# SSD exponentials queued behind ScalarE's last evacuation, and modulation rows in buffers of their own

## The chip, the core and the metric

One NeuronCore of a Trainium2 chip runs the whole kernel. Its engines are TensorE (PE, matrix products; PEld is its weight load), VectorE (DVE), ScalarE (ACT), GpSimd (POOL) and SyncE (SP, which here only issues DMAs). Each works through its own queue in order and waits on semaphores of the others. The metric is the device time of one execution in microseconds (us), less is better.

## The reference

Two layers over 512 latent and 256 context tokens of width 1024. Layer 0 mixes tokens by gated linear attention (GLA), layer 1 by a Mamba-2 scan (SSD) with 8 groups of 4 heads; each is followed by a squared-ReLU MLP (FFN), and each sub-layer is modulated by shift, scale and gate that come from the conditioning vectors.

```python
def sq_relu_mlp(h, w1, w2):
    return jnp.square(jax.nn.relu(h @ w1)) @ w2

def ssd_chunk_scan(xs, dt, a, bm, cm, s0):
    ...
    def step(s, inp):
        xi, dti, bi, ci = inp
        cum = jnp.cumsum(dti * a, axis=1)
        seg = cum[:, :, None] - cum[:, None, :]
        decay = jnp.exp(jnp.where(mask, seg, -jnp.inf))
        xdt = xi * dti[..., None]
        cb = jnp.einsum('bign,bjgn->bijg', ci, bi)
        y = jnp.einsum('bijg,bijgr,bjgrp->bigrp', cb, decay, xdt)
        y = y + jnp.einsum('bign,bigr,bgrpn->bigrp', ci, jnp.exp(cum), s)
        ...

def reference(...):
    ...
    s_lat = jax.nn.silu(c)
    s_ctx = jax.nn.silu(c_ctx)
    for i in range(DEPTH):
        m_l = jnp.split((s_lat @ ada_w[i] + ada_b[i])[:, None, :], 6, axis=-1)
        m_c = jnp.split(s_ctx @ ada_w[i] + ada_b[i], 6, axis=-1)
        ul = snake(modulate(hl, m_l[0], m_l[1]))
        ...
        hl = layer_norm(DEEPNORM_ALPHA * hl + m_l[2] * snake(yl), ln_g[i, 0], ln_b[i, 0])
        hl = layer_norm(DEEPNORM_ALPHA * hl + m_l[5] * sq_relu_mlp(modulate(hl, m_l[3], m_l[4]), ffn_w1[i], ffn_w2[i]),
                        ln_g[i, 1], ln_b[i, 1])
```

## The kernel before

Activations stand transposed, 128 features to a partition and up to 768 tokens along a row. A large product (`prod`, L250) splits both operands in a high and a low part and adds three products, so one output block of 128 features takes 8 slices of depth times 3 matmuls for each token segment. A block's weights come by a DMA of 512 KB into a raw tile (`wload`, L237), ScalarE casts the high part (L203, `wh`) and VectorE subtracts for the low part (L204, `wl`). The raw tiles are one pool of four buffers.

A scheduler orders the instructions of each engine when the kernel is built, by the order of the program and by when it expects operands to be ready; on the chip every engine keeps that order. Two lists of generators are woven into the products: `worked()` counts the columns that `prod` has sent, and every 768 of them it makes a step of `side`, and every `pace[0]` such units a step of `background`.

The **background** work is `ada_rows`. For a modulation vector (layer, m) it takes eight blocks; for each it loads 512 KB of the modulation weights (L154) into a raw tile, and VectorE multiplies it by the conditioning row and sums along the row (L157), twice where context and latent tokens both need it (the first result then goes to a junk tile). These raw tiles were taken from the weights' four buffers. 24 such loads belong to the GLA stage and 56 to the first FFN.

The **FFN** runs in blocks of eight hidden slices: `f1` makes a product, ScalarE takes the relu out of PSUM (L394) and squares it (L396), GpSimd squares it in full precision (L395, `rq`), VectorE subtracts (L397, `rl`); then `accum_proj` makes eight products of the block with the second weight matrix and VectorE adds each to the accumulators (L431). The gate for that addition comes from the rows.

The **SSD** layer runs over eight groups. For a group, `group(g)` makes the products of B, C and two x blocks, each followed by `conv` (evacuation of PSUM by ScalarE at L887 and L889, start of the conv at L894, four taps on VectorE at L896, tanh at L898), then two gate products (`gate_tiles`, tanh at L919). The scan of the group before (`inner`) is a `side` generator and goes in between. It

- copies B and x to natural layout by transposes (L906) and copies on ScalarE (L907, `Bn`, `xnat`);
- weights x with the decays on VectorE (L961, `xw`) and makes chunk states (L973), and the C-B products with a copy on ScalarE (L995, `cbs`);
- loads decay rows for a chunk of 128 tokens and both directions (L939, tile `L`, ten buffers), masks them on GpSimd (L941), takes 4 exponentials on each tile on ScalarE (L1028, function `decays`), adds both directions on GpSimd (L1031), multiplies by `cbs` on VectorE (L1032) and makes the outputs on TensorE (L1039).

The loads, masks and exponentials depend on nothing of the group but its decay rows, so the scheduler was free to place them far ahead.

Of the kernel before, what the change touches and what calls it, by code (L numbers as in the profile page):

```python
# [9 lines left out]
F32 = mybir.dt.float32  # L10
# [6 lines left out]
P = 128  # L17
D = 1024
# [42 lines left out]
def tile_backbone(ctx, tc, xT, cc, cr, vecs, rows, ada_w0, ada_wr, lnf, ffn_w1, ffn_w2,  # L61
# [81 lines left out]
    def ada_rows(items, alloc, junk):  # L143
        srow = [alloc(s) for s in range(2)]
        for s in range(2):
            nc.sync.dma_start(srow[s], cr[s:s + 1, :].to_broadcast([P, D]))
            nc.scalar.activation(srow[s], srow[s], AF.Silu)
        for layer, m in items:
            streams = range(1 if layer and m > 1 else 2)
            t = ct([P, 8, 2], f"row{layer}{m}")  # L150
            nc.gpsimd.memset(t, 0.0)
            for b in range(8):
                raw = raw_tile()
                nc.sync.dma_start(raw, ada_wr[48 * layer + 8 * m - 16 + b])  # L154
                for s in streams:
                    o = raw if s == streams[-1] else junk()
                    nc.vector.scalar_tensor_tensor(o, raw, 1.0, srow[s], ALU.mult, ALU.mult, accum_out=t[:, b, s:s + 1])  # L157
                yield
            c0 = V_ADA + 48 * layer + 8 * m
            nc.vector.tensor_tensor(t, t, vec[:, c0:c0 + 8].unsqueeze(2).to_broadcast([P, 8, 2]), ALU.add)  # L160
            mods[layer, m] = t
# [211 lines left out]
    def ffn(layer, xs, acc, segs, pool, npre, presegs, restsegs, passes, after):  # L373
        W1, W2 = ffn_w1[layer], ffn_w2[layer]
        rs = {}
        NN = span(segs)[1]

        def f1(m, sg, hold=None):
            w, ps = hold or (weights(W1, m), mm_ps(sg))
            prod(ps, w, xs, sg, KT)  # L380
            f1_out(m, ps)

        def f1_out(m, ps):
            if m not in rs:
                rs[m] = (pool.tile([P, NN], F32R, tag="rs", name=nm("rh"), bufs=20),
                         pool.tile([P, NN], F32R, tag="rs", name=nm("rl"), bufs=20))
            rh, rl = rs[m]
            for piece in passes if m == DFF // P - 1 else (segs,):
                a, b = span(piece)
                eng = nc.gpsimd if piece is segs else nc.vector  # L390
                r = pool.tile([P, NN], F32, tag="rr", name=nm("rr"), bufs=2)
                q = pool.tile([P, NN], F32, tag="rq", name=nm("rq"), bufs=1)
                for (t0, n, _) in piece:
                    nc.scalar.activation(r[:, t0:t0 + n], part_of(ps, t0, n), AF.Relu)  # L394
                eng.tensor_mul(q[:, a:b], r[:, a:b], r[:, a:b])  # L395
                nc.scalar.activation(rh[:, a:b], r[:, a:b], AF.Square)  # L396
                nc.vector.tensor_sub(rl[:, a:b], q[:, a:b], rh[:, a:b].bitcast(F32))  # L397

        nlast = NN // 256
        h0 = 0  # L400
        for bi, nb in enumerate((8, 8, 8, 8 - nlast, nlast)):
            ms = range(h0, h0 + nb)
            if bi == 0:
                drain(1)
                held = []
                for m in ms[:npre]:
                    held.append((weights(W1, m), mm_ps(segs)))
                    prod(held[-1][1], held[-1][0], xs, presegs, KT)
                drain()
                for m in ms[:npre]:  # L410
                    f1(m, restsegs, held[m])
                pace[0] = 11
                ms = ms[npre:]
            if bi == 4:
                ws = pair_weights(W2, h0, nb,
                                  lambda j: [pool.tile([P, NN], F32R, tag="rs", name=nm("ws"), bufs=20) for _ in range(2)])
            for m in ms:
                f1(m, segs)
            ys = [rs[m] for m in range(h0, h0 + nb)]
            if bi == 0:  # L420
                gate = mod(layer, 5)
                pace[0] = 22
            if bi < 4:
                accum_proj(W2, h0, nb, ys, gate, acc, segs)
            else:
                accum_last(ws, ys, gate, acc, passes, after, early=None if layer == 0 else 5)
            h0 += nb
# [44 lines left out]
    def gla_layer(xs, first):  # L472
# [17 lines left out]
        def wk(shape, name):  # L490
            return gp.tile(shape, F32, tag="wk", name=nm(name), bufs=3)

        background.append(ada_rows([(0, 2), (0, 3), (0, 4)], lambda s: xn_tile(f"srow{s}"), raw_tile))
        pace[0] = 12
        aT = gp.tile([P, NT], F32R, tag="aT", name="aT")
        a2 = gp.tile([P, 2, 512], F32R, tag="a2", name="a2")
# [265 lines left out]
    def ssd_layer(xs, accd, acc0):  # L762
# [117 lines left out]
        def conv(j, segs):  # L880
            ps = held[1] if j == 16 else project(16 + j, segs)
            pre = pres[0]
            pres.reverse()
            c = sp.tile([P, NT + 2], F32, tag="cv", name=nm("cv"), bufs=1)
            f = apool.tile([P, NT], F32, tag="acc", name=nm("cf"))
            n = 512 if len(segs) == 1 else NT + 2
            nc.scalar.copy(pre[:, 2:514], ps[0])  # L887
            if len(segs) > 1:
                nc.scalar.copy(pre[:, 516:772], ps[1][:, 0:NCTX])  # L889

            def cw(t):
                return cvec[:, 32 * t + j:32 * t + j + 1]

            nc.scalar.activation(c[:, 0:n], pre[:, 2:2 + n], AF.Identity, bias=cw(5), scale=cw(2))  # L894
            for t in (0, 1, 3, 4):
                nc.vector.scalar_tensor_tensor(c[:, 0:n], pre[:, t:t + n], cw(t), c[:, 0:n], ALU.mult, ALU.add)  # L896
            for t0, t1, d in ((0, 512, 0), (512, 768, 2)) if len(segs) > 1 else ((0, 512, 0),):
                nc.scalar.activation(f[:, t0:t1], c[:, t0 + d:t1 + d], AF.Tanh)  # L898
                nc.vector.scalar_tensor_tensor(f[:, t0:t1], f[:, t0:t1], 1.0, c[:, t0 + d:t1 + d], ALU.add, ALU.mult)
            return f  # L900

        def natural(f, dst):
            for c0, c1 in ((0, 4), (4, 6)):
                pt = sm_ps([P, 4, P])
                for c in range(c0, c1):
                    nc.tensor.transpose(pt[:, c - c0, :], f[:, c * P:(c + 1) * P], ident)  # L906
                nc.scalar.copy(dst[:, c0:c1, :], pt[:, 0:c1 - c0, :])  # L907

        def group(g):
            fB = conv(16 + g, BOTH)  # L910
# [4 lines left out]
            def gate_tiles():  # L915
                for i in range(2):
                    z = sp.tile([P, NL], F32, tag="zs", name=nm("zs"), bufs=4)
                    zp = project(2 * g + i, LAT)[0]
                    nc.scalar.activation(z, zp, AF.Tanh, scale=0.5)  # L919
                    nc.vector.scalar_tensor_tensor(z, z, 1.0, zp, ALU.add, ALU.mult)  # L920
                    zs.append(z)

# [4 lines left out]
        def inner(g, fB, fC, fx, zs):  # L927
# [119 lines left out]
            for c in range(NLC + 1):  # L1047
# [2 lines left out]
                    outputs(c - 1, Ms.pop(c - 1))  # L1050
                if c < NLC:
                    L = Rs.pop(c)
                    decays(c, L)
                    Ms[c] = masks(c, L)
                if c + 2 < NLC:
                    Rs[c + 2] = chunk_rows(c + 2)
# [268 lines left out]
```

## Time and profile before

| | us |
|---|---|
| median of 3 runs (lowest to highest) | 1975.5 (1969.12 to 1980.79) |
| the profiled execution | 1972.94 |
| its span, first to last instruction | 1971.2 |
| TensorE busy in the span | 1882.0 |
| VectorE, ScalarE, GpSimd busy | 1260.5, 801.5, 414.6 |
| mean granted TensorE clock | 0.985 |

In a row of the profile `L1028 ACT ACTIVATE L<-L,lcol ... x4 [3.94 <-POOL L L941]` four instructions of line 1028 ran on ScalarE, which had stood idle for 3.94 us before them until line 941 on GpSimd had written tile L. PEclk is the clock that TensorE was granted, as a share of full speed. A DMA's time goes from issue to landing. By time the stages are about: the start and GLA to 450 us, the first FFN to 1050, the SSD layer to 1590, and the second FFN.

### The profile page before, as it was taken

What the parts mean: (1) busy time and instruction counts of PE and PEld (TensorE: products, weight loads), DVE (VectorE), ACT (ScalarE), POOL (GpSimd) and SP (SyncE); (2) the same over time, 40 slices, a digit from 0 to 9 for tenths busy, and PEclk for the clock granted to TensorE, in tenths of its full rate; (3) what the DMA queues carried; (4) which work ended last, traced back from release to release, by engine and by line L of the source; (5) the groups of instructions that cost most, each with busy time, mean ns of one, the idle gap of its engine ahead of it and who ended that gap; (6) DMA issues with size and microseconds to landing.
All of it is one profiled execution on the core that took longest, in us unless ns stands there. A gap on an engine that the chain in (4) does not pass through costs nothing.

```text
span 1971.2 us, 28815 instructions
## 1 busy us (share of the span) xinstructions
PE 1882.0 (95%) x11365; PEld 1607.1 (82%) x11365; DVE 1260.5 (64%) x1932; ACT 801.5 (41%) x1387; POOL 414.6 (21%) x363
## 2 busy tenths in 40 slices
PE   7989999999999999999998799999999999999997
PEld 5978888788788888888987677777787788888886
DVE  4797887888854444324478778787897673333335
ACT  3435456454213113122367645565443453323231
POOL 1123241202002002010004523334221221102012
PEclk9999999999999999999999899999999999999999
DMA  8423213124654444213134333344324423333321
GB/s 327 153 62 122 87 57 104 48 72 129 202 150 140 129 134 131 70 46 108 44 109 119 129 116 97 102 133 134 97 90 137 146 81 104 97 98 97 98 83 63
DMA packets 78999, 219.07 MB, mean 111 GB/s; under 512 B 11088, under 2 KB 15824, under 8 KB 78864
## 3 DMA queue, kind: packets, MB, share of 16 engines
q1 hardware_dynamic: 78864, 217.24, 35.3%
q8 instruction: 89, 1.46, 0.3%
q14 instruction: 46, 0.38, 0.1%
HBM read 209.07 MB, written 8.13 MB: 110 GB/s over the span
## 4 chain that ended last, share of the span: by engine, by line
PE 63%; DVE 15%; ACT 6%; issue 5%; DMA 5%; POOL 5%; SPq 0%; DVEq 0%; POOLq 0%; ACTq 0%
PE mm L250 54%; DMA L<-crowc 3%; DVE cv L896 2%; POOL L L1031 1%; DVE A L605 1%; PE sm L973 1%; DVE wl L204 1%; PE sm L688 1%; DVE E L616 1%; DVE raw L157 1%; PE mm L532 1%; ACT xn L325 1%; ACT wh L203 1%; ACT L L1028 1%; DVE lnst L315 1%
## 5 line engine op out<-in xcount | busy, mean ns | idle before, releaser
L250 PE MATMUL mm<-xh,wl 128*128 128x512 f32 (+1 forms) x1800 | 545.6, 356 | 8.3 <-DVE wl L204 8.3
L250 PE MATMUL mm<-xh,wh 128*128 128x512 f32 (+1 forms) x1800 | 548.8, 359 | 1.3 <-ACT xh L1073 1.1
L250 PE MATMUL mm<-xl,wh 128*128 128x512 f32 (+1 forms) x1800 | 546.1, 356 | 2.4 <-DVE xl L1074 2.4
L203 ACT CAST wh<-raw 128x1024 fp32r<-128x1024 f32 (+3 forms) x225 | 226.1, 1006 | 642.7 <-PE mm L250 590.6
L204 DVE TENSOR_TENSOR wl<-raw,wh 128x1024 fp32r<-128x1024 f32 (+3 forms) x225 | 276.0, 1228 | 166.8 <-ACT wh L203 163.5
L250 PEld LDWEIGHTS mm<-xh,wl 128*128 128x128 f32 x1800 | 300.9, 190 | 57.6 <-DVE wl L204 9.9
L250 PEld LDWEIGHTS mm<-xh,wh 128*128 128x128 f32 x1800 | 301.8, 190 | 53.1 <-issue 4.5
L250 PEld LDWEIGHTS mm<-xl,wh 128*128 128x128 f32 x1800 | 300.6, 190 | 52.1 <-DVE xl L1074 4.3
L395 POOL TENSOR_TENSOR rq<-rr 128x768 f32<-128x768 f32 (+1 forms) x62 | 104.7, 1689 | 735.3 <-ACT rr L394 731.4
L250 PE MATMUL mm<-rl,wh 128*128 128x512 f32 x704 | 212.5, 355 | 4.0 <-DVE rl L397 4.0
L250 PE MATMUL mm<-rh,wl 128*128 128x512 f32 x704 | 212.3, 355 | 0.0
L250 PE MATMUL mm<-rh,wh 128*128 128x512 f32 x704 | 212.0, 354 | 0.0
L431 DVE SCALAR_TENSOR_TENSOR acc<-mm,row,acc 128x256 f32<-128x256 f32 (+1 forms) x182 | 100.7, 580 | 164.1 <-PE mm L250 163.7
L157 DVE SCALAR_TENSOR_TENSOR raw<-raw,srow 128x1024 f32<-128x1024 f32 x104 | 128.7, 1242 | 85.7 <-DMA raw<-in_ada_wr_dram 84.9
L896 DVE SCALAR_TENSOR_TENSOR cv<-pre,cvec,cv 128x770 f32<-128x770 f32 (+1 forms) x128 | 135.9, 1062 | 13.0 <-ACT cv L894 11.4
L250 PEld LDWEIGHTS mm<-rl,wh 128*128 128x128 f32 x704 | 116.3, 189 | 23.3 <-DVE rl L397 4.3
L250 PEld LDWEIGHTS mm<-rh,wl 128*128 128x128 f32 x704 | 116.5, 189 | 19.0
L250 PEld LDWEIGHTS mm<-rh,wh 128*128 128x128 f32 x704 | 116.3, 188 | 19.0
L1028 ACT ACTIVATE L<-L,lcol 128x128 f32<-128x128 f32 x256 | 81.7, 392 | 64.9 <-POOL L L941 64.9
L397 DVE TENSOR_TENSOR rl<-rq,rh 128x768 fp32r<-128x768 f32 (+2 forms) x67 | 53.2, 795 | 70.7 <-POOL rq L395 69.1
L941 POOL TENSOR_SCALAR_AFFINE_SELECT L<-L 128x512 f32<-128x512 f32 x64 | 57.2, 898 | 167.3 <-DMA L<-crowc 165.4
L898 ACT ACTIVATE cf<-cv 128x512 f32<-128x512 f32 (+1 forms) x56 | 27.6, 533 | 85.7 <-DVE cv L896 85.5
(295 smaller groups left out, 2536.1 us busy)
## 6 DMA issues: line engine op xcount, KB each, us to landing
raw<-in_ffn_w_dram SPq DMA_DIRECT2D x112, 512.0 KB, 3.7
raw<-in_ada_wr_dram SPq DMA_DIRECT2D x80, 512.0 KB, 3.7
raw<-in_ssd_w_in_dram SPq DMA_DIRECT2D x48, 512.0 KB, 3.9
L<-crowc SPq DMA_DIRECT2D x64, 256.0 KB, 3.6
raw<-in_ada_w_dram SPq DMA_DIRECT2D x16, 512.0 KB, 9.2
raw<-in_gla_w_in_dram SPq DMA_DIRECT2D x16, 512.0 KB, 3.5
ec<-crow SPq DMA_DIRECT2D x64, 128.0 KB, 3.0
acc<-in_xT_dram SPq DMA_DIRECT2D x14, 384.0 KB, 6.9
```

Source lines behind the costliest of these rows:

```text
L157: nc.vector.scalar_tensor_tensor(o, raw, 1.0, srow[s], ALU.mult, ALU.mult, accum_out=t[:, b, s:s + 1])
L203: nc.scalar.copy(h, src)
L204: nc.vector.tensor_sub(l, src, h.bitcast(F32))
L250: nc.tensor.matmul(part_of(ps, t0, n), a[:, k, :], b[:, t0:t0 + n], start=(k == 0 and i == 0), stop=(k == kt - 1 and i == 2))
L315: nc.vector.bn_stats(st[:, h], ps)
L395: eng.tensor_mul(q[:, a:b], r[:, a:b], r[:, a:b])
L397: nc.vector.tensor_sub(rl[:, a:b], q[:, a:b], rh[:, a:b].bitcast(F32))
L431: nc.vector.scalar_tensor_tensor(acc[m][:, t0:t0 + n], part_of(ps, t0, n), gate[:, m, s:s + 1], (src or acc)[m][:, t0:t0 + n], ALU.mult, A ...
L896: nc.vector.scalar_tensor_tensor(c[:, 0:n], pre[:, t:t + n], cw(t), c[:, 0:n], ALU.mult, ALU.add)
L898: nc.scalar.activation(f[:, t0:t1], c[:, t0 + d:t1 + d], AF.Tanh)
L941: nc.gpsimd.affine_select(out=L[z], in_=L[z], compare_op=ALU.is_ge, fill=NEG, base=0, pattern=[[0, 4], [1 - 2 * z, P]], channel_multiplier ...
L1028: nc.scalar.activation(t[:, h, :], t[:, h, :], AF.Exp, bias=lcol[:, c, r:r + 1])
```

## The change

The rows get a tag of their own with three buffers (`rawa`, 12 KB of each partition), and each row's load is issued one row ahead; a first load stands ahead of the loop with a yield behind it. The pace of the background in the first block of the FFN goes from 11 to 15. GLA's junk tile moves to the new tag as well. In the SSD layer the evacuations at L887, L907 and L919 are remembered in `evac`, and the exponentials of a chunk are issued inside `tc.issue_after(...)`, which makes the scheduler put them behind the remembered instruction on their engine; this is an edge of order only, on the same engine.

```diff
+        def load(layer, m, b):
+            raw = wpool.tile([P, D], F32, tag="rawa", name=nm("rawa"), bufs=3)
+            nc.sync.dma_start(raw, ada_wr[48 * layer + 8 * m - 16 + b])
+            return raw
+
+        todo = [(layer, m, b) for layer, m in items for b in range(8)]
+        raws = [load(*todo.pop(0))]
+        yield
         for layer, m in items:
...
             for b in range(8):
-                raw = raw_tile()
-                nc.sync.dma_start(raw, ada_wr[48 * layer + 8 * m - 16 + b])
+                if todo:
+                    raws.append(load(*todo.pop(0)))
+                raw = raws.pop(0)
...
-                pace[0] = 11
+                pace[0] = 15
...
-        background.append(ada_rows([(0, 2), (0, 3), (0, 4)], lambda s: xn_tile(f"srow{s}"), raw_tile))
+        background.append(ada_rows([(0, 2), (0, 3), (0, 4)], lambda s: xn_tile(f"srow{s}"), lambda: wpool.tile([P, D], F32, tag="rawa", name=nm("junk"), bufs=3)))
...
-            nc.scalar.copy(pre[:, 2:514], ps[0])
+            evac[0] = nc.scalar.copy(pre[:, 2:514], ps[0])
...
+        evac = [None]
+
         def natural(f, dst):
...
-                nc.scalar.copy(dst[:, c0:c1, :], pt[:, 0:c1 - c0, :])
+                evac[0] = nc.scalar.copy(dst[:, c0:c1, :], pt[:, 0:c1 - c0, :])
...
-                    nc.scalar.activation(z, zp, AF.Tanh, scale=0.5)
+                    evac[0] = nc.scalar.activation(z, zp, AF.Tanh, scale=0.5)
...
-                    decays(c, L)
+                    with tc.issue_after(evac[0].ins):
+                        decays(c, L)
```

On ScalarE, at the turn to the second group's scan (the same `cbs_10415` in both), the exponentials of later groups (`L_11410`, `L_11419`) stood between the natural copies before:

```order
695 L907 COPY xnat_10318<-sm_10331 128x4x128
696 L907 COPY xnat_10318<-sm_10337 128x2x128
697 L1028 ACTIVATE L_11410<-L_11410,lcol 128x128 x4
698 L907 COPY xnat_10318<-sm_10355 128x4x128
699 L907 COPY xnat_10318<-sm_10361 128x2x128
700 L1028 ACTIVATE L_11419<-L_11419,lcol 128x128 x4
701 L995 COPY cbs_10415<-sm_10410 128x512
```

Now the copies run through, and the group's own first exponentials (`L_10297`) stand behind the evacuation of the C conv (`pre_9454<-mm_10468`); the changed kernel's line numbers are 9 to 12 higher:

```order
672 L918 COPY xnat_10318<-sm_10355 128x4x128
673 L918 COPY xnat_10318<-sm_10361 128x2x128
674 L1006 COPY cbs_10415<-sm_10410 128x512
675 L212 CAST wh_10650<-raw_10648 128x1024
676 L896 COPY pre_9453<-mm_10283 128x512
677 L898 COPY pre_9453<-mm_10284 128x256
678 L903 ACTIVATE cv_10449<-pre_9453,cvec 128x770
679 L907 ACTIVATE cf_10450<-cv_10449 128x512
680 L907 ACTIVATE cf_10450<-cv_10449 128x256
681 L896 COPY pre_9454<-mm_10468 128x512
682 L1039 ACTIVATE L_10297<-L_10297,lcol 128x128 x4
683 L903 ACTIVATE cv_10523<-pre_9454,cvec 128x512
```

What moved: exponentials for groups two further on gave way to those of the group itself, some ten places later.

On SyncE, whose queue issues the loads, at the start of the first FFN, weights (`in_ffn_w`) and rows (`in_ada_wr`) took turns before:

```order
102 L237 DMA raw_4709<-in_ffn_w_dram 128x1024
103 L154 DMA raw_4725<-in_ada_wr_dram 128x1024
104 L154 DMA raw_4752<-in_ada_wr_dram 128x1024
105 L146 DMA srow_4583<-in_cr_dram 128x1024
106 L146 DMA srow_4584<-in_cr_dram 128x1024
107 L237 DMA raw_4784<-in_ffn_w_dram 128x1024
108 L154 DMA raw_4796<-in_ada_wr_dram 128x1024
```

Now:

```order
105 L246 DMA raw_4851<-in_ffn_w_dram 128x1024
106 L246 DMA raw_4926<-in_ffn_w_dram 128x1024
107 L246 DMA raw_5001<-in_ffn_w_dram 128x1024
108 L146 DMA srow_4583<-in_cr_dram 128x1024
109 L146 DMA srow_4584<-in_cr_dram 128x1024
110 L150 DMA rawa_4761<-in_ada_wr_dram 128x1024
111 L150 DMA rawa_4813<-in_ada_wr_dram 128x1024
112 L150 DMA rawa_4865<-in_ada_wr_dram 128x1024
```

What moved: seven weight loads (four more stand ahead of these) now go out before the row loads of this piece, of which the first three had gone out earlier.

On VectorE, in the accumulation of the FFN's first block, from one product's accumulation (L431) to the next, before:

```order
600 L431 SCALAR_TENSOR_TENSOR acc_3243<-mm_5491,row_4589,acc_3243 128x512
601 L431 SCALAR_TENSOR_TENSOR acc_3243<-mm_5492,row_4589,acc_3243 128x256
602 L204 TENSOR_TENSOR wl_5682<-raw_5679,wh_5681 128x1024
603 L157 SCALAR_TENSOR_TENSOR raw_5922,row_5728<-raw_5922,srow_4583 128x1024
604 L431 SCALAR_TENSOR_TENSOR acc_3958<-mm_5554,row_4589,acc_3958 128x512
```

and now:

```order
604 L440 SCALAR_TENSOR_TENSOR acc_3239<-mm_5407,row_4654,acc_3239 128x512
605 L440 SCALAR_TENSOR_TENSOR acc_3239<-mm_5408,row_4654,acc_3239 128x256
606 L213 TENSOR_TENSOR wl_5601<-raw_5598,wh_5600 128x1024
607 L166 SCALAR_TENSOR_TENSOR rawa_6453,row_6451<-rawa_6453,srow_4583 128x1024
608 L166 SCALAR_TENSOR_TENSOR rawa_6510,row_6451<-rawa_6510,srow_4583 128x1024
609 L166 SCALAR_TENSOR_TENSOR rawa_6567,row_6451<-rawa_6567,srow_4583 128x1024
610 L166 SCALAR_TENSOR_TENSOR rawa_6624,row_6451<-rawa_6624,srow_4583 128x1024
611 L440 SCALAR_TENSOR_TENSOR acc_3242<-mm_5470,row_4654,acc_3242 128x512
```

What moved: four row operations stand between two accumulations, where one stood before; the rows are through earlier.

## The prediction

> **What bounds the kernel now.** I read the page's busy table first, then the chain that ended last, then TensorE's waits, and then the stretches in which those waits lie.
>
> ```profile
> span 1971.2 us, 28815 instructions
> PE 1882.0 (95%) x11365; PEld 1607.1 (82%) x11365; DVE 1260.5 (64%) x1932; ACT 801.5 (41%) x1387; POOL 414.6 (21%) x363
> PE 63%; DVE 15%; ACT 6%; issue 5%; DMA 5%; POOL 5%; SPq 0%; DVEq 0%; POOLq 0%; ACTq 0%
> ```
>
> TensorE (PE) is the bound: idle for only 1971.2 − 1882.0 = 89 us. What a change to the other engines can win is in that idle time, and in time at a lowered clock behind it. TensorE's waits, by what ended them:
>
> ```profile
> PE sm L973 <- DVE xw L961: 14.6, 6, 3.5
> PE sm L1039 <- issue: 8.6, 1, 8.6
> PE sm L586 <- DVE E L616: 8.3, 10, 3.3
> PE mm L250 <- DVE wl L204: 8.3, 5, 3.6
> PE mm L250 <- DVE rl L397: 4.0, 1, 4.0
> PE sm L715 <- ACT on L693: 3.2, 3, 2.3
> ```
>
> The columns are total us, times, longest. The first two lie in the SSD groups, L204 and L397 in the first FFN, L586 and L715 in the GLA. The stretches (us, busy time and instructions of each engine, granted clock, DMA share, GB/s): seven group periods from the first copy of the C-B products (L995) to the eighth, one such period alone, the start of the first FFN in two pieces, and the GLA stage.
>
> ```profile
> core 0: us, PE busy (x) PEld busy (x) DVE busy (x) ACT busy (x) POOL busy (x), PEclk, DMA share, GB/s
> 1069.17:1502.23 433.06, 403.32 (x2215) 325.30 (x2213) 354.97 (x523) 228.39 (x476) 146.80 (x109) 0.97 0.36 113
> 1386.84:1442.81 55.97, 55.97 (x319) 45.95 (x319) 49.20 (x72) 29.07 (x58) 17.09 (x12) 1.00 0.35 109
> 448.00:525.00 77.00, 69.35 (x406) 60.81 (x405) 69.03 (x109) 27.88 (x47) 16.49 (x8) 0.97 0.54 172
> 525.00:575.00 50.00, 50.00 (x285) 44.04 (x284) 30.62 (x50) 5.93 (x6) 0.00 (x0) 0.98 0.55 163
> 60.00:450.00 390.00, 368.77 (x2902) 328.66 (x2901) 322.40 (x512) 202.93 (x328) 97.31 (x94) 0.99 0.28 87
> ```
>
> A mean group takes 433.06/7 = 61.9 us; the second row is a group that had no wait and full clock, 55.97 us, with VectorE (DVE) at 49.20 as second bound. So there is a floor near 56 us, and the kernel has already reached it once.
>
> **Part 1: the exponentials behind an evacuation.** Rows of ScalarE (ACT), then VectorE and TensorE, at a steady group's turn:
>
> ```profile
> 1137.08 1.28 ACT L1028 ACTIVATE L<-L,lcol 128x128 f32<-128x128 f32 x4 [3.94 <-POOL L L941]
> 1138.26 0.83 ACT L907 COPY xnat<-sm 128x512 f32<-128x512 f32 x2
> 1139.12 2.60 DVE L961 TENSOR_TENSOR xw<-xnat,wc 128x256 f32<-128x256 f32 x6 [6.24 <-ACT xnat L907]
> 1140.53 2.07 PE L973 MATMUL sm<-xw,Bn 128*128 128x512 f32 x3 [3.32 <-DVE xw L961]
> ```
>
> Four exponentials of a group further on stand ahead of a natural-layout copy, wait 3.94 us for their masked tile from GpSimd (POOL), and the copy, the six products of VectorE and TensorE's L973 wait in a row behind them. At the first group it is a pile:
>
> ```profile
> 1086.68 1.28 ACT L1028 ACTIVATE L<-L,lcol 128x128 f32<-128x128 f32 x4 [4.66 <-POOL L L941]
> 1090.02 1.28 ACT L1028 ACTIVATE L<-L,lcol 128x128 f32<-128x128 f32 x4 [2.06 <-POOL L L941]
> 1093.44 0.99 ACT L1028 ACTIVATE L<-L,lcol 128x128 f32<-128x128 f32 x3 [2.14 <-POOL L L941]
> 1095.16 0.56 ACT L887 COPY pre<-mm 128x512 f32<-128x512 f32 x1
> 1098.27 1.12 PE L1039 MATMUL sm<-L,xnat 128*64 128x128 f32 x8 [8.60 <-issue]
> ```
>
> Each set waits for its own tile, the evacuation of the conv product (L887) waits behind them all, and TensorE stands 8.60 us. The change ties every exponential of the group under work behind the evacuation issued last; the new order has the natural copies and the C-B copy in one run and the exponentials behind the evacuation of the C conv. Both waits lose their cause: 14.6 + 8.6 = 23.2 us. The clock went with them: (1 − 0.97) × 433.06 = 13.0 us. Together **−36.2 us**, leaving (433.06 − 36.2)/7 = 56.7 a group, the floor that the gapless group shows.
>
> What the clock charges, and from which gap on, is in two rows more, a piece with a gap of 1.72 us and one with gaps of 0.69 and 2.34:
>
> ```profile
> 1126.00:1136.00 10.00, 8.28 (x55) 7.22 (x53) 6.53 (x6) 6.28 (x16) 7.75 (x5) 1.00 0.40 128
> 163.50:173.50 10.00, 6.97 (x34) 5.93 (x34) 7.32 (x13) 4.05 (x10) 3.31 (x3) 0.83 0.42 148
> ```
>
> 1.72 us left the clock at 1.00; 2.34 us cost (1 − 0.83) × 10 = 1.7 us more. So a gap above about 2.3 us costs itself and 1.7 or more. [...]
>
> What is late next? The moved exponentials now sit on the way to the first outputs (L1039) of their group. From the end of the C conv's product the way is: evacuation, 4 exponentials, the conv's start (L894), 4 exponentials, the add on GpSimd, the mask on VectorE. The rows (groups of instructions from 1145 to 1442 us, shapes kept apart; total us and mean ns of one, then idle time ahead):
>
> ```profile
> L887 ACT COPY pre<-mm 128x512 f32<-128x512 f32 x20 | 11.5, 576 | 0.0
> L894 ACT ACTIVATE cv<-pre,cvec 128x512 f32<-128x512 f32 x5 | 4.1, 819 | 4.7 <-DVE cf L899 4.7
> L1031 POOL TENSOR_TENSOR L<-L,L 128x512 f32<-128x512 f32 x19 | 32.6, 1714 | 16.8 <-ACT L L1028 16.8
> L1032 DVE TENSOR_TENSOR L<-L,cbs 128x512 f32<-128x512 f32 x20 | 13.6, 681 | 0.0
> L898 ACT ACTIVATE cf<-cv 128x512 f32<-128x512 f32 x20 | 12.7, 633 | 67.4 <-DVE cv L896 67.4
> ```
>
> 0.58 + 1.28 + 0.82 + 1.28 + 1.71 + 0.68 = 6.35 us, and about 7.4 with the tanh of the B conv (0.63 and 0.4 for its short half) ahead on ScalarE. In the new order 40 matmuls of the next conv cover it: a product of 48 matmuls at full rate takes 8.3 us (later pieces of the FFN hold 290 matmuls in 50 us, 0.172 each), so 40 take 6.9 us. The wait is between 0 and, if VectorE is late with its taps too, 1.5 us a group. I take 0.5, since the sum of rows is within 0.5 of the cover at both ends: +3.5 over seven groups, **SSD −32.7**, bounds −36.2 and −36.2 + 7 × 1.5 = −25.7. VectorE also waits at that mask and has 56 − 49.2 = 6.8 us a group to spare for it. GpSimd's adds of T (L1018) now stand ahead of the adds of L, and SyncE's loads of L fall later, into buffers that have been free for a group; both are inside the sum above. If this cover is gone, each us of chain costs 7.
>
> In the last group nothing follows for the exponentials to hide under but the output product; 0 to 3 us, inside the bounds.
>
> **Part 2: rows with buffers of their own, pace 15.** In the first FFN, weights and modulation rows shared four buffers, and the casts of weights (L203) waited for loads issued late, with relu evacuations (L394) behind:
>
> ```profile
> 473.10 1.05 ACT L203 CAST wh<-raw 128x1024 fp32r<-128x1024 f32 x1 [6.31 <-DMA raw<-in_ffn_w_dram]
> 469.39 1.01 PE L250 MATMUL mm<-xh,wl 128*128 128x512 f32 x2 [3.63 <-DVE wl L204]
> 523.57 1.01 PE L250 MATMUL mm<-rl,wh 128*128 128x512 f32 x2 [4.02 <-DVE rl L397]
> ```
>
> In the new order seven weight loads go out ahead of the rows and the weight's subtraction (L204) stands two places earlier on VectorE. Both waits go: 3.63 + 4.02, and the clock, 0.03 × 77 + 0.02 × 50 = 3.3: −10.95 at most. Against it, the rows are now bunched: four to a product in the accumulation, where before it was one. Their prices:
>
> ```profile
> L157 DVE SCALAR_TENSOR_TENSOR raw<-raw,srow 128x1024 f32<-128x1024 f32 x104 | 128.7, 1242 | 85.7 <-DMA raw<-in_ada_wr_dram 84.9
> L431 DVE SCALAR_TENSOR_TENSOR acc<-mm,row,acc 128x256 f32<-128x256 f32 (+1 forms) x182 | 100.7, 580 | 164.1 <-PE mm L250 163.7
> L204 DVE TENSOR_TENSOR wl<-raw,wh 128x1024 fp32r<-128x1024 f32 (+3 forms) x225 | 276.0, 1228 | 166.8 <-ACT wh L203 163.5
> DMA to landing us min/median/max: 3.4/3.7/9.8
> GB/s 0 96 306 389 412 415 426 404 393 413 410 403 413 399 410 406 400 414 408 404 412 408 395 401 416 406 415 407 147 14 0 0 5 66 284 0 106 243 0 11
> ```
>
> VectorE's work to a product is 4 × 1.24 + 2 × 0.58 + 1.23 = 7.35 us, under TensorE's 8.3. But with three buffers the fourth row's load starts when the first row is done: 1.24 + load + 1.24 + 2.39 = 4.87 + load, so 8.6 us at the median load (fourth line, the rows' loads) and 9.9 at 5.0. Over eight products VectorE slips 2 or 13 us, of which a second PSUM set covers one product, 8.3. So 0 to 5 us come back; four rows and a weight, 5 × 0.524 MB in 8.3 us, are 316 GB/s, where the core's first 60 us moved 400 and more (last line, 40 slices), so a load should stay near its median and I take 3: **−8**, bounds −11 and 0.
>
> [...]
>
> In the GLA the rows come earlier (the first of them ahead of the level products that L586 waits for) and its junk tile leaves the weights' buffers. The waits there are 8.3 + 3.2 with (1 − 0.99) × 390 = 3.9 of clock. Fewer weight waits can win up to half of that, −7; two or three rows of 1.24 us put ahead of the end of a scan can cost 3 and the clock, +5. I take **−2**, nearer the middle of these. The added yield and the second tag issue nothing more: the same 80 loads and 104 row operations.
>
> **The sum**: 1972.94 (profiled time, 2.6 under the median of 1975.5) − 32.7 − 8 − 2 = **1930 us**.
>
> **Rivals.**
> (a) The wait moves: the exponentials come too late and L1039 waits in every group. For it: the cover and the chain are equal within 0.5 us, with three engines in the chain. A gap of 3.5 us and 1.7 of clock in seven groups, 36.4, cancels the whole SSD gain: 1972.94 + 0.2 − 10 = 1963. It becomes **slower than before** when the gap passes (36.2 + 10)/7 − 1.7 = 4.9, a chain of 11.8 us; at a gap of 6.5 the time is 1972.94 − 46.2 + 57.4 = 1984. That needs GpSimd's add to stand behind a select that waits for its load, as the select here does:
>
> ```profile
> 1169.22 1.47 POOL L941 TENSOR_SCALAR_AFFINE_SELECT L<-L 128x512 f32<-128x512 f32 x1 [8.77 <-DMA L<-crowc]
> ```
>
> Against it: in the new order the first two adds stand ahead of the next selects.
> (b) The rows' loads slow down in the bunch: at 9.2 us each a product takes 14.1 us of VectorE, 8 × 5.8 − 8.3 = 38 us late, against −32.7 − 2: 1976, no change. The longest row load, 9.8, was at the kernel's crowded start; it decides at 8.8 us.
> (c) The edges don't bind and the exponentials stay early: only part 2 acts, 1972.94 − 10 = 1963. Against it: the new order shows them moved.
>
> **How the numbers follow.** Forecast, 1912 to 1946: 0.80. (a) in part, or (c), 1947 to 1963: 0.11. (b) or (a) near break-even: 0.05. (a) in full: 0.04. The range goes from 1910 (all waits gone, GLA at −7, small gaps too) to 1962, the partial rivals. Half a per cent, 10 us, is about what a measurement of this kernel can tell from no change: faster 0.91, same 0.05, slower 0.04.
>
> **What would show it.** Right: L973 behind L961 and the 8.6 at L1039 vanish, the group period is 56 to 58, PEclk 0.99 or more over the seven periods, and the two gaps at L204 and L397 are gone. Wrong: waits of L1039 or L250 behind L1032 or POOL L1031 over 2 us in each group; PE busy under 50.0 of 50 us in the first FFN's accumulation, with VectorE idle ahead of the row operations; longer waits at L715.

## The result

The changed kernel takes 1946.54 us (median of 4, 1946.12 to 1946.91) against 1977.61 before: a ratio of 0.9849, 95% interval 0.9817 to 0.9882. In a later run of both on one chip it was 1954.49 (1952.32 to 1955.86) against 1977.94, a ratio of 0.9882 (0.9840 to 0.9924); what differs between the two is told below. Faster was forecast, and 1930 us with a range of 1910 to 1962; the gain between the profiled executions is 1972.94 − 1946.43 = 26.5 us where 43 was forecast.

The page of the changed kernel, its busy table and its chain:

```profile
span 1944.7 us, 28804 instructions
PE 1870.5 (96%) x11365; PEld 1596.9 (82%) x11365; DVE 1265.5 (65%) x1932; ACT 797.8 (41%) x1387; POOL 411.6 (21%) x363
PE 59%; DVE 22%; issue 6%; ACT 5%; DMA 4%; POOL 3%; SPq 1%; DVEq 0%; ACTq 0%; POOLq 0%
```

TensorE is still the bound, and VectorE's share of the chain has grown from 15 to 22%. The waits of TensorE after that bear on the argument (total us, times, longest; the changed kernel's L1050 is the outputs, L406 the rl subtraction):

```profile
PE sm L1050 <- DVE L L1043: 9.1, 6, 1.5
PE sm L595 <- DVE E L625: 7.0, 10, 1.7
PE mm L259 <- DVE rl L406: 5.4, 1, 5.4
PE mm L259 <- DVE acc L440: 3.2, 3, 1.6
PE sm L1050 <- issue: 2.4, 1, 2.4
PE mm L259 <- DVE wl L213: 2.1, 3, 1.1
PE sm L724 <- ACT on L702: 1.8, 1, 1.8
```

The 14.6 us behind `xw` are gone, and 8.6 us at the first outputs have become 2.4. In their place each of the six later groups waits 1.5 us at its first outputs, behind the mask on VectorE. The wait for `wl` has shrunk to small ones, the one for `rl` has grown from 4.0 to 5.4. The stretches after: the seven SSD group periods, one of them, and three pieces of the first FFN:

```profile
core 0: us, PE busy (x) PEld busy (x) DVE busy (x) ACT busy (x) POOL busy (x), PEclk, DMA share, GB/s
1064.09:1473.23 409.14, 393.42 (x2213) 320.27 (x2212) 358.97 (x521) 234.23 (x505) 140.35 (x111) 1.00 0.39 121
1122.32:1180.29 57.97, 56.00 (x319) 45.72 (x318) 50.34 (x75) 32.02 (x70) 20.70 (x16) 1.00 0.39 118
470.00:521.00 51.00, 45.65 (x255) 39.61 (x254) 51.00 (x72) 14.40 (x21) 10.28 (x5) 0.94 0.65 207
521.00:571.00 50.00, 50.00 (x288) 43.65 (x287) 41.26 (x71) 6.17 (x6) 0.00 (x0) 0.99 0.79 255
571.00:621.00 50.00, 48.13 (x274) 41.41 (x274) 38.66 (x59) 11.86 (x18) 9.13 (x4) 1.00 0.76 247
```

A group takes 57.97 us, of which TensorE is busy for 56.00. In the FFN from 470 to 521 us VectorE is busy for all of the 51 us.

Where the time went, between points that both traces have (the wait of 1.60 us for the accumulator at the end of the GLA, the first step product of the SSD layer, the first and the eighth `cbs` copy, the end):

| stage | before, us | after, us | change | forecast |
|---|---|---|---|---|
| to the end of the GLA | 429.53 | 425.79 | −3.7 | −2 |
| first FFN, to the SSD's first step product | 592.23 | 593.07 | +0.8 | −8 |
| to the first `cbs` copy | 47.41 | 45.23 | −2.2 | 0 |
| seven SSD group periods | 433.06 | 409.14 | −23.9 | −32.7 |
| the rest | 468.97 | 471.47 | +2.5 | 0 |

So two terms failed to come in full: 9 us each in the FFN and in the SSD groups. The seven periods were 75.9, 61.3, 60.9, 58.6, 61.0, 56.0 and 59.4 us before and are 58.2, 58.0, 57.9, 58.0, 57.7, 57.7 and 61.7 after: 17.7 of the 23.9 us come from the first one, and the last two grew.

### The profile page after: what moved, and what is told of

Same layout as the page of the kernel before. It is cut to its first block, busy times and chain, and to the rows that moved or that the text cites. A ratio compares the mean times of both kernels' runs of the same rounds, so it can differ in the third digit from the quotient of the medians.

```text
span 1944.7 us, 28804 instructions
## 1 busy us (share of the span) xinstructions
PE 1870.5 (96%) x11365; PEld 1596.9 (82%) x11365; DVE 1265.5 (65%) x1932; ACT 797.8 (41%) x1387; POOL 411.6 (21%) x363
## 4 chain that ended last, share of the span: by engine, by line
PE 59%; DVE 22%; issue 6%; ACT 5%; DMA 4%; POOL 3%; SPq 1%; DVEq 0%; ACTq 0%; POOLq 0%
PE mm L259 51%; DVE cv L905 3%; DVE wl L213 2%; DMA rawa<-in_ada_wr_dram 2%; DVE junk L166 2%; DVE rawa L166 2%; DVE cf L908 2%; DVE A L614 1%; PE sm L697 1%; POOL W L633 1%; PE mm L541 1%; DMA raw<-in_ada_w_dram 1%; DVE acc L440 1%; ACT wh L212 1%; DVE E L625 1%
## 5 line engine op out<-in xcount | busy, mean ns | idle before, releaser
L213 DVE TENSOR_TENSOR wl<-raw,wh 128x1024 fp32r<-128x1024 f32 (+3 forms) x225 | 272.1, 1211 | 198.2 <-ACT wh L212 194.3
L404 POOL TENSOR_TENSOR rq<-rr 128x768 f32<-128x768 f32 (+1 forms) x62 | 106.8, 1722 | 734.1 <-ACT rr L403 675.7
L440 DVE SCALAR_TENSOR_TENSOR acc<-mm,row,acc 128x256 f32<-128x256 f32 (+1 forms) x182 | 100.7, 580 | 205.3 <-PE mm L259 204.9
L905 DVE SCALAR_TENSOR_TENSOR cv<-pre,cvec,cv 128x770 f32<-128x770 f32 (+1 forms) x128 | 146.1, 1141 | 14.5 <-ACT cv L903 12.8
L166 DVE SCALAR_TENSOR_TENSOR rawa<-rawa,srow 128x1024 f32<-128x1024 f32 x80 | 101.0, 1278 | 17.9 <-DMA rawa<-in_ada_wr_dram 17.4
L406 DVE TENSOR_TENSOR rl<-rq,rh 128x768 fp32r<-128x768 f32 (+2 forms) x67 | 53.2, 794 | 65.3 <-POOL rq L404 65.0
L907 ACT ACTIVATE cf<-cv 128x512 f32<-128x512 f32 (+1 forms) x56 | 27.6, 533 | 92.5 <-DVE cv L905 92.5
```

The costliest lines, as they stand in the source:

```text
L213: nc.vector.tensor_sub(l, src, h.bitcast(F32))
L440: nc.vector.scalar_tensor_tensor(acc[m][:, t0:t0 + n], part_of(ps, t0, n), gate[:, m, s:s + 1], (src or acc)[m][:, t0:t0 + n], ALU.mult, A ...
```

## The experiments

**Each part alone.** The first kernel has the old rows and the new order of exponentials, the second the new rows only:

```diff
 # the kernel before, with the evacuations remembered, and
+                    with tc.issue_after(evac[0].ins):
+                        decays(c, L)
 # the changed kernel, and
-                    with tc.issue_after(evac[0].ins):
-                        decays(c, L)
+                    decays(c, L)
```

> Part 1 alone (exponentials behind the last evacuation, rows as before). Theory A, the two parts add up: the seven SSD group periods sum to about 409 us as with the whole change (433 before), the first FFN keeps the waits of 3.6 at the weight subtraction and 4.0 at rl, and the time is 1973 - 24 + 0 to 2 of tail = about 1950. Rival B, the parts help each other (rows out of the way of the SSD stage): the periods sum to over 415 and the time is over 1956.

> Part 2 alone (rows in their own buffers, pace 15, exponentials free). Theory A: the SSD starts 5 us earlier than before, as with the whole change, its seven periods sum to about 433 with the 3.3 us waits at L973, and the time is about 1968. Rival B: SSD periods differ by over 5 us from 433.

Measured: 1959.18 and 1978.81 us beside 1975.79 of the kernel before. The seven periods of each (the first row is the exponentials alone):

```profile
1076.73:1486.87 410.14, 392.64 (x2213) 318.99 (x2212) 360.05 (x521) 234.33 (x505) 133.75 (x111) 1.00 0.39 121
```

```profile
1071.50:1506.80 435.30, 406.86 (x2215) 328.12 (x2213) 357.80 (x523) 228.40 (x477) 138.10 (x109) 0.96 0.35 112
```

410.14 and 435.30: the gain of the SSD groups belongs to the order of the exponentials alone, and the rows add nothing there. Theory A holds for these periods. Both totals were 9 and 11 us above its numbers, though, 1950 and 1968, and with the rows alone the SSD layer's first step product came at 1023.4 us, not 5 us ahead of the 1021.8 before. The stage of the first FFN was longer in both (600.1 and 598.3 us against 592.2), and no wait accounts for it; that led to the next question.

**A pace that no wait shows.** From 650 to 900 us TensorE has no gap in any of these kernels. The same stretch of the kernel before, of the changed kernel, and of the exponentials alone:

```profile
650.00:900.00 250.00, 250.00 (x1445) 220.44 (x1444) 92.42 (x123) 53.95 (x73) 23.62 (x14) 1.00 0.33 98
```

```profile
650.00:900.00 250.00, 250.00 (x1444) 218.56 (x1443) 66.83 (x79) 52.29 (x71) 23.09 (x14) 1.00 0.20 60
```

```profile
650.00:900.00 250.00, 250.00 (x1417) 216.69 (x1416) 88.93 (x119) 52.22 (x71) 22.81 (x13) 1.00 0.32 97
```

All are busy for 250 of 250 us at a clock of 1.00, and yet the third ran 1417 matmuls where the others ran 1444 or 1445: a pair of 512 and 256 columns takes 2 × 250/1417 = 0.353 us instead of 0.346. To tell whether that belongs to the kernel, the changed kernel and the exponentials alone were run once more, unaltered:

> The changed kernel once more, unaltered. In the looks so far a pair of matmuls (512 and 256 columns) in the gapless part of the first FFN, 600 to 900 us, took 347 ns in three kernels (the one before, the changed one, the anchor on B) and 353 ns in three others (the two parts alone, the rows held), which is 8 us over the FFN. Theory F, it is a property of an execution, not of the kernel: this run may show either pace, and the times of one kernel spread by up to 8 to 10 us. Theory G, it belongs to the kernel: 347 again, and 1946.5 within 1 us.

> Part 1 alone again, timed. By F its times lie between 1950 and 1960 and a profile may show 347 ns a pair; by G it shows 353 and 1959. In both the seven SSD periods sum to 410.

The changed kernel, the same code, now took 1954.49 us, and its profiled execution (1955.86 us) showed 1417 in that stretch:

```profile
650.00:900.00 250.00, 250.00 (x1417) 216.93 (x1416) 65.76 (x76) 52.75 (x72) 23.56 (x14) 1.00 0.20 58
```

So theory G falls for the changed kernel: the same code has shown both paces. The exponentials alone were between 1950.37 and 1962.52 in four runs, their periods 410.0 again, and their profile stayed at 0.353, which G allows too; but in the table below a kernel with the same FFN code shows 0.346, and one with the FFN code of the kernel before shows 0.353. The FFN's code does not fix the pace, then, as theory F has it. Nor does the chip alone: one showed 0.346 with the exponentials one conv earlier (below) and 0.353 with each part alone, and another showed both in the last table of this section. Whether it is set anew in each execution is not shown, because only one execution of a run has a profile.

In the first trace of the changed kernel the pairs start 0.347 us apart at full clock from 470 us on, 0.353 from a gap of TensorE of 0.82 us that ends at 579.55 to one of 1.05 that ends at 589.40, and 0.347 again from there to 950 us. In the trace of before they start 0.347 apart at full clock from 470 to 950 us, on both sides of a gap of 4.02. The pace is worth some 8 us: the stage of the FFN took 592.2 us in the kernel before, at 0.346, and 600.1 in the same FFN code at 0.353. Between the two profiled executions of the changed kernel it is 5.8 of 9.4 us; the GLA has 1.9 and the SSD groups 1.5 of the rest. So totals below are compared at one pace, called by the length of its pair, 0.346 or 0.353.

**The wait for rl in the FFN.** Each row operation of the first FFN is held on VectorE behind the last rl subtraction or accumulation issued before it, and the pace is 20:

```diff
-                    nc.vector.scalar_tensor_tensor(o, raw, 1.0, srow[s], ...)
+                    with tc.issue_after(rlast[0].ins) if rlast[0] else ExitStack():
+                        nc.vector.scalar_tensor_tensor(o, raw, 1.0, srow[s], ...)
...
-                nc.vector.tensor_sub(rl[:, a:b], q[:, a:b], rh[:, a:b].bitcast(F32))
+                rlast[0] = nc.vector.tensor_sub(rl[:, a:b], q[:, a:b], rh[:, a:b].bitcast(F32))
...
-                pace[0] = 15
+                pace[0] = 20
```

> The whole change, with each row operation of the first FFN held on VectorE behind the last rl subtraction or accumulation issued before it, pace 20 instead of 15: two row operations to a product instead of five or six. Theory A, VectorE was saturated there (51.0 of 51 us): the 5.4 us wait for rl and its clock loss of 3.4 go, the waits of 0.8 and 1.1 in the accumulation too, the time is 1946.5 - 8.8 to 10.6 = 1936 to 1938. Rival E, the single rq buffer between GpSimd and VectorE sets the rl: the wait stays above 3 us.

> The rows held, again, timed. Its waits in the first FFN stay gone. By F the times lie between 1938 and 1948; by G at 1947 with 353 ns a pair.

First the changed kernel's own rows, VectorE and then TensorE ahead of the wait:

```profile
507.37 0.95 DVE L406 TENSOR_TENSOR rl<-rq,rh 128x768 fp32r<-128x768 f32 x1
508.24 1.21 DVE L166 SCALAR_TENSOR_TENSOR rawa<-rawa,srow 128x1024 f32<-128x1024 f32 x1
509.38 2.48 DVE L166 SCALAR_TENSOR_TENSOR junk<-rawa,srow 128x1024 f32<-128x1024 f32 x1
...
515.23 1.21 DVE L213 TENSOR_TENSOR wl<-raw,wh 128x1024 fp32r<-128x1024 f32 x1
...
516.45 0.95 DVE L406 TENSOR_TENSOR rl<-rq,rh 128x768 fp32r<-128x768 f32 x1
```

```profile
517.46 1.01 PE L259 MATMUL mm<-rl,wh 128*128 128x512 f32 x2 [5.36 <-DVE rl L406]
```

and GpSimd beside the slow row operation:

```profile
508.46 2.32 POOL L404 TENSOR_TENSOR rq<-rr 128x768 f32<-128x768 f32 x1 [7.83 <-DVE rl L406]
```

Between two rl subtractions VectorE runs five row operations, one of them at 2.48 us instead of 1.21, and never idles: 516.45 − 507.37 = 9.1 us for a product that TensorE makes in 8.3. The slow one began while GpSimd was squaring the relu (L404), and ended at 511.86, 1.08 us after GpSimd at 510.78; the row operation before it, begun 0.22 us ahead of GpSimd's, took its usual 1.21. VectorE's rl subtractions from 469.02 us on begin 9.0 to 10.2 us apart, so that it falls behind with each product until TensorE wants the last rl and stands. With the rows held the same stretch reads:

```profile
470.00:521.00 51.00, 51.00 (x291) 44.27 (x290) 35.03 (x51) 14.38 (x21) 8.69 (x5) 1.00 0.51 158
```

TensorE has no gap, its clock is 1.00, and VectorE is at 35 us. Theory A holds for the waits, and rival E falls: the single rq buffer is unchanged and there is no wait. The hold and the pace of 20 came together; which of them it takes was not tried. The time was 1947.12 and then 1947.05 (1946.21 to 1948.15), not the 1936 to 1938 expected, and both profiles had 0.353 us a pair; the changed kernel with that pair on the same chip was 1954.49, so holding the rows is worth 7.4 us there, all of it in the stage of the FFN (591.4 us against 598.9). All four profiles with rows held, of three kernels, showed 0.353, and no kernel of them had times 8 us apart; whether holding the rows favours the slower pace was not tried, and if it does, these 7.4 us are given back: the changed kernel at 0.346 took 1946.54.

**The wait of the outputs.** First the exponentials of a group's first chunks were put one conv earlier:

```diff
-            evac[0] = nc.scalar.copy(pre[:, 2:514], ps[0])
+            e = nc.scalar.copy(pre[:, 2:514], ps[0])
+            if 16 <= j < 24:
+                evac[0] = e
```

> The whole change, but only the evacuation of the B conv (and natural copies and gates) is remembered, so the first exponentials stand one conv earlier on ScalarE. Theory A, the 1.5 us wait of the outputs in each group is the chain evacuation of C, exponentials, conv start, exponentials, add, mask: the wait falls under 0.3, the group period to 56.4, the time to 1946.5 - 7 x 1.5 = 1936. Rival C, VectorE's three taps ahead of the mask set it: the wait stays above 1.0 and the time above 1942. Rival D, the earlier exponentials delay the conv's evacuations: a new wait at the natural transposes.

1945.28 us, and the outputs still wait: 3.4 us at the first, 1.4 to 1.8 in each group after it. Rival D's new wait does not show; the transposes wait 3.8 us for VectorE in place of 3.5. GpSimd's adds, then VectorE, in this kernel (its L1044, L1031, L1032 and L1045 are the add of L, the addition of T, the step after it, and the mask):

```profile
1127.19 1.47 POOL L1044 TENSOR_TENSOR L<-L,L 128x512 f32<-128x512 f32 x1 [15.04 <-ACT L L1041]
1132.47 1.29 POOL L1031 TENSOR_TENSOR T<-T,ec 128x512 f32<-128x512 f32 x1
```

```profile
1133.80 1.75 DVE L1032 SCALAR_TENSOR_TENSOR T<-cf,dcol,T 128x512 f32<-128x512 f32 x1 [2.16 <-POOL T L1031]
1140.67 0.68 DVE L1045 TENSOR_TENSOR L<-L,cbs 128x512 f32<-128x512 f32 x1
```

The tile was ready at 1128.7 and masked at 1140.67: it is VectorE's queue that is late, and VectorE itself waits for GpSimd's T. Theory A falls; C holds in that VectorE sets the wait, though not by its taps alone. In the changed kernel the same is seen on VectorE and GpSimd:

```profile
1136.43 2.12 DVE L908 SCALAR_TENSOR_TENSOR cf<-cf,cv 128x512 f32<-128x512 f32 x2
1139.50 3.24 DVE L905 SCALAR_TENSOR_TENSOR cv<-pre,cvec,cv 128x512 f32<-128x512 f32 x3 [0.28 <-ACT cv L903]
1142.66 0.68 DVE L1043 TENSOR_TENSOR L<-L,cbs 128x512 f32<-128x512 f32 x1
```

```profile
1136.60 1.67 POOL L1029 TENSOR_TENSOR T<-T,ec 128x512 f32<-128x512 f32 x1 [3.00 <-DVE ec L1028]
1140.72 1.47 POOL L1042 TENSOR_TENSOR L<-L,L 128x512 f32<-128x512 f32 x1 [2.44 <-ACT L L1039]
```

Two tanh products take 2.12 us beside GpSimd's T, and 1.01 in the run below, where T is not GpSimd's; the second of them, 128x256, takes 1.52 us here and 0.41 to 0.42 at the eight places of this trace where no operation of GpSimd overlaps it. Of three taps, 3.24 us together, the last begins during GpSimd's add, takes 1.67 us where the first two take 0.75 each, and ends 0.55 us after it (1140.72 + 1.47 = 1142.19). So the addition of T went to VectorE, with the rows held:

```diff
-                nc.gpsimd.tensor_add(T[:, i], T[:, i], E)
+                nc.vector.tensor_add(T[:, i], T[:, i], E)
```

> The rows held and, in the SSD scan, the addition of the two directions' inter-chunk terms (T, two a group) moved from GpSimd to VectorE. Theory C, the outputs' wait of 1.5 us is VectorE's queue ahead of the mask: it waits 1.2 us for GpSimd's T and runs its two-input operations at half speed beside it (2.12 us for two tanh products of 1.06). Then the wait falls to 0.5 or less, the group period from 57.8 to 56.6 or less, and the time is 7 to 8 us under that of the rows held. Theory A, the chain on ScalarE sets it: the wait stays at 1.2 or more. Rival H, two more operations of 0.68 us fill VectorE and the period grows.

1935.91 us (1934.90 to 1936.72), 11 under the rows held at the same pace, more than the 7 to 8 expected. VectorE and TensorE at the same place, and the seven periods:

```profile
1132.05 1.01 DVE L911 SCALAR_TENSOR_TENSOR cf<-cf,cv 128x512 f32<-128x512 f32 x2
1137.48 0.68 DVE L1046 TENSOR_TENSOR L<-L,cbs 128x512 f32<-128x512 f32 x1
```

```profile
1138.88 0.66 PE L1053 MATMUL sm<-L,xnat 128*64 128x128 f32 x8
```

```profile
1062.75:1462.11 399.36, 392.30 (x2213) 318.73 (x2212) 371.36 (x534) 234.66 (x505) 115.45 (x97) 1.00 0.40 124
```

But for 0.8 us at the first, the outputs no longer wait, although VectorE has 371 us of work in place of 359 and is 93% busy; six of the periods are 56.0 to 56.6 us, the seventh 61.6. Theory A and rival H fall. The edit takes two things away at once, VectorE's wait for T and the work of GpSimd beside VectorE's; what each gives was not tried.

**What each edit is worth beside the others.** T on VectorE with the change as it is, with the exponentials alone, with the last group's exponentials left free, and in the kernel before:

> The whole change with T's addition on VectorE, rows not held. If T's addition is all that the outputs waited for: seven SSD periods sum to 399 as with the rows held, no wait of the outputs over 0.5, the wait for rl in the first FFN stays at 5.4, and the time is 10 to 11 under the changed kernel's at the same pace of the FFN's matmuls: 1936 at 347 ns a pair, 1944 at 353.

> Part 1 and T's addition on VectorE, rows as before. The SSD periods sum to 399 to 400; the GLA ends 4 us later than with part 2 and the first FFN keeps waits of 3.6 and 3.5 us: 1941 at 347 ns a pair, 1949 at 353. If part 2 is worth nothing at equal pace, within 2 us of e9.

> Rows held, T on VectorE, and in the last group the exponentials free to go early, as before. Theory A, the seventh period (61.6 to 63 against 59.4 before) is longer because the last group's exponentials stand behind its natural copies and the casts of the output product: it returns to about 59.5 and the time falls by 2 (1934 at 353 ns a pair). Rival, the period is long because VectorE's tanh products and weight subtractions queue there: unchanged.

> The kernel before with only T's addition on VectorE. Theory A, the order of the exponentials is needed first: the waits at L973 of 3.3 us and the pile at the first outputs stay, the periods sum to over 425, the time is within 6 us of the kernel before. Rival I, GpSimd was the cause all along, since it serves the selects later for T: the periods fall under 410.

| kernel | median, us (range) | seven periods | a pair in the profiled FFN |
|---|---|---|---|
| the change, T on VectorE | 1939.46 (1934.75 to 1948.56) | 400.4 | 0.353 |
| exponentials alone, T on VectorE | 1950.22 (1941.15 to 1951.34) | 401.0 | 0.346 |
| rows held, T on VectorE, last group free | 1940.08 (1937.81 to 1941.72) | 404.9 | 0.353 |
| before, T on VectorE | 1967.02 (1958.94 to 1981.20) | 430.9 | 0.353 |

The first two nearly as expected: profiled, 1942.15 at 0.353 and 1941.15 at 0.346, with a wait of 1.9 us left at the first outputs of the change. So part 2 is worth some 7 us at equal pace by these two, of which the GLA has 5 (its end, the 1.60 us wait, at 424.9 and 430.3), and 3 to 7 by the changed kernel and the exponentials alone at 0.353 (1955.86 against 1959.18 and 1962.52). The third was a miss for A: the seventh period stayed at 62.9 and the time did not fall, so the last group's order is not the cause of its length; what the rival names, VectorE's queue, was not tried. In the kernel before, T alone gives a ratio of 0.9957 (0.9934 to 0.9980), 7 us where 6 at most were expected, but the waits of the exponentials stay: the one at `xw` is smaller, the pile at the first outputs larger:

```profile
PE sm L1039 <- issue: 13.1, 1, 13.1
PE sm L973 <- DVE xw L961: 10.4, 5, 3.7
```

Rival I falls, and the order of the exponentials had to come first. The best of all is the rows held with T on VectorE: 1935.91 us, a ratio of 0.9791 (0.9756 to 0.9826) to the kernel before, and that at 0.353 in its profile.

## Why the prediction was right, and where it was short

- **Part 1, the waits that go.** Right, and shown by the first experiment: L973's 14.6 and 6.2 of the 8.6 at the first outputs went, the clock over the seven periods rose from 0.97 to 1.00, and the order of the exponentials alone brings 433.06 to 410.1.
- **Part 1, what is late next.** The step was right in its place, the first outputs, and wrong in its size: "I take 0.5" a group, measured 1.5, the upper bound, for which the prediction had no row; that the bound was met is partly luck. The sum of the rows, 6.35 to 7.4 us, counted each operation at its mean and let VectorE's mask start when its tile was ready. The runs show VectorE's queue instead: it waits for GpSimd's addition of T (1.18 us at 1133.64 in the changed kernel), a tanh product and a tap that began during an operation of GpSimd took 1.52 and 1.67 us where others took 0.42 and 0.75, and the mask stands behind them. "GpSimd's adds of T now stand ahead of the adds of L" was named there and said to be inside the sum, which has no term for it. Six groups at 1.5 and 2.4 at the first, in place of 3.5, are 8.0 us more than was priced. The clock was priced too high as well: TensorE's busy time in the seven periods fell by 9.9 us (403.32 to 393.42) and not by 13.0, because 5.7 of the 27.3 us of half clock lay inside waits, which had their own price (4.68 in the wait of 8.60, 1.05 in one of 3.51 that began at 1377.84). Smaller waits that fell by 2.3 us take the rest, so that the SSD groups lack 8.8.
- **The floor near 56 us** was not reached with the change: the group of 55.97 took 57.7. It was reached when T moved to VectorE.
- **Rival (a)** is what came, in its mildest form. Its break-even of 4.9 us a gap was far off.
- **Part 2, "Both waits go".** This step failed. The wait for wl of 3.6 us went; the one for rl grew to 5.4, and two of 0.8 and 1.1 in the accumulation came new. Half clock came with that wait, and with the wait of 1.60 us at the end of the GLA too, where the kernel before kept full clock:

```profile
517.46:521.96 4.50, 4.50 (x14) 3.82 (x15) 4.50 (x9) 1.05 (x1) 0.00 (x0) 0.50 0.65 218
425.79:429.80 4.01, 4.01 (x20) 3.91 (x21) 2.72 (x10) 2.87 (x5) 0.82 (x2) 0.57 0.00 0
```

That is 2.2 and 1.7 us of work lost, both booked under the FFN. Together 11.2 us came in place of the 10.95 that were to be won, which is 0.3 of the 0.8 us that the stage grew by. I priced the bunched rows in the accumulation, where a row is one operation, and not in the products before it, where a row is two: five operations, one of them of 2.48 us beside GpSimd's squaring, are more than a product's time (9.1 us against 8.3). The held rows show it. The price that was set for the accumulation, 0 to 5 us, held: 1.9.
- **Part 2, the loads.** Weights were no longer late, as said; the loads of the rows did not become the bound (rival b): they took 4.7 us in the median from 440 to 640 us, inside the 3.7 to 5.0 of the sum, over 521 to 621 us the rate was 247 to 255 GB/s, and TensorE lacked 1.9 us.
- **GLA**: −3.7 against −2, within its bounds: the waits at the level products fell from 8.3 to 7.0 and the longest from 3.3 to 1.7, so that the clock no longer fell inside the stage. In the nine profiles with the new rows it ends at 424.9 to 428.0 us, in the five with the old ones at 429.5 to 431.1.
- **The clock rule** read from two rows, a loss above 2.3 us only, does not hold. After the change the gap of 2.4 us at the first outputs cost no clock, nor did gaps of 1.77 and 1.80 in the GLA, while a gap of 1.86 us in the first stretch below and one of 1.51 in the second did:

```profile
1456.00:1466.00 10.00, 8.14 (x38) 6.49 (x37) 8.95 (x13) 7.39 (x16) 5.58 (x2) 0.83 0.90 284
1576.00:1588.00 12.00, 9.81 (x64) 8.94 (x63) 8.54 (x25) 8.68 (x18) 1.08 (x2) 0.86 0.00 1
```

They cost 1.7 us each; the first lies in the seventh period, the second is most of what the rest lost. By these rows the length of one gap does not tell what it costs. Half clock began at 1460.62 and at 1583.50, and in the 3.41 us ahead of each (the step of the last section) TensorE was busy for less than half, in the second with two more gaps of 0.34 us:

```profile
1457.20:1460.62 3.42, 1.56 (x12) 1.23 (x11) 2.92 (x4) 3.33 (x7) 3.34 (x2) 1.00 0.86 250
1580.09:1583.50 3.41, 1.64 (x11) 1.27 (x12) 0.59 (x4) 3.16 (x5) 0.54 (x1) 1.00 0.00 0
```

- **The total** of 1946.5 us lies just past the upper end of the 1912 to 1946 that had most of the chance, and 1954.5 in the band that was set for rival (a) in part. Which pace the FFN runs at, a spread that was not foreseen, moves it by some 8 us either way. The profile of before and the first one of after have the same pace, so that the stages above compare like with like.

## What to carry to other kernels

When an instruction is put off, the time for it is not the sum of the operations on its way but the place that it and they have in each engine's queue: look on every engine of the way for what stands ahead and what that waits for. A background task that a pace or a buffer shortage held back can be pulled forward by the scheduler once it has buffers of its own; price it at its most expensive form and in the stage that it lands in, and tie it down by an order edge if that stage has no room. Moving a short operation from a lightly used engine to a busy one can pay, when the busy one waits for it and takes longer beside it: here the two tanh products took 2.12 us with the operation on GpSimd and 1.01 with it on VectorE, VectorE went from 359 to 371 us of work, and the seven group periods fell from 410.1 to 399.4 us.

## What was not expected of the hardware

- Two paces of the same gapless matmuls at a clock of 1.00: 1444 or 1417 in 250 us, 1.9%, in executions of the same code. In the trace of before one of them, 0.347 us a pair, held from 470 to 950 us, and in the first of the changed kernel it changed twice, at gaps of 0.82 and 1.05 us. What sets it stays open; nothing was tried against it.
- A row operation of VectorE and a squaring of GpSimd that overlap: the one begun second ended last, by nearly the same time in every pair. In the first FFN of the changed kernel seven row operations begun during a squaring (L404) took 1.87 to 2.50 us, each ending 1.08 us after it, while nine begun ahead of one took their usual 1.21 to 1.23, and there the squaring ended 1.32 to 1.33 us after them. The accumulations (L440, 128x256) took 0.43 to 0.48 us at the 22 places of that trace where an operation of GpSimd of over 0.1 us overlapped, and 0.43 to 0.49 at the 98 others.
- In the changed kernel's trace half clock begins, up to 1915 us, at 426.39, 515.13, 1051.03, 1460.62 and 1583.50 us, which are whole multiples of 3.413 us apart, and lasts for 3.41 us or twice that. In the trace of before its ten starts up to there are such multiples apart too, and it lasts for 3.41 to 10.24 us. Counted in such steps over these two traces, from 100 to 1915 us, each of the 13 steps at full clock in which TensorE was busy for under 45% (0 to 39%) was followed by half clock; of six with 45 to 49% two were, and of those with 50% and more none.
